# Inverting the 32x32 blocks of the WKV recurrence: the substitution on Pool over 128 partitions in place of VectorE in two halves

## The chip, the cores and the metric

The kernel runs on one core of a Trainium2 chip. Its engines are TensorE (PE, matrix products), VectorE (DVE), ScalarE (ACT), GpSimd (called Pool in the profile) and SyncE (SP), which here only issues DMAs. The metric is the device time of one execution in microseconds; the median of several runs is compared.

## The reference, cut to what matters

The kernel computes two blocks of a network on 1024 tokens of width 1024. The second block has, beside an attention branch and gates, a recurrence (WKV) over 8 heads of 64 channels. For each head a 64x64 state is carried over the tokens:

```python
def step(state, inp):
    r_t, d_t, k_t, v_t, a_t, b_t = inp
    sa = jnp.einsum('bhvk,bhk->bhv', state, a_t)
    state = (state * d_t[:, :, None, :] + sa[..., None] * b_t[:, :, None, :]
             + v_t[..., None] * k_t[:, :, None, :])
    return state, jnp.einsum('bhvk,bhk->bhv', state, r_t)
...
_, ys = lax.scan(step, jnp.zeros((B, H, N, N), jnp.float32), xs)
```

## The kernel before

All matrices are float32. Large products are made of three products each (`mm3`, L139 to L141): a weight is split into a high part by ScalarE (L103) and a low part by VectorE (L104). The weights go through two buffers each (`wr`, `wh`, `wl`), so that one unit of such a product (48 matmuls of 128x512) needs one load, one cast and one split.

The recurrence is computed in chunks of 64 tokens, and four chunks of all 8 heads make a time block; there are four time blocks, `tb` = 0 to 3. The function `rwkv` (L954) steps through generators. For each block, `wkv_prep` loads the inputs, scales them, normalises the keys (L1011 to L1021, with a reciprocal on VectorE at L1015) and multiplies them into 64x128 matrices `at` (L1114, masked at L1116). `wkv_inverse` inverts the 64x64 triangular part of each, first its 32x32 diagonal blocks: 32 pairs of head and chunk with two diagonal blocks each. `wkv_chain` then carries the state through the four chunks (L1193 to L1213), and `wkv_out` (L1225 to L1231) finishes.

The diagonal blocks go through DRAM (`dg`, stored at L1119), so that they can be loaded with one block's matrix in each partition: `d` and `tt` hold 128 partitions, one for a block, and matrix entries along the free axis. Each block is inverted by substitution in 31 steps; step j takes one product (L1144, into `tmp`) and one sum (L1145, into `tt`). The step works on n x m entries for each partition, with n = j // 2 + 1 and m = 31 - j; each step needs the one before. Partitions 0 to 63 and 64 to 127 have instructions of their own (`q` = 0 and 1). The results go back through DRAM (L1147), a transposed copy (`tn`, L1148) through `t11` (L1150), and are loaded at L1155 and L1159 into the layout that TensorE's products take (L1168 and L1174).

While a block is prepared and inverted, TensorE has other work: `projections` makes the latents and 16 gates (21 units of products of `hn`, into DRAM `cl` and `gd`). It follows the loop in the program; the functions' order in the program is a priority, and a planner that knows a cost for each instruction lays out a fixed order for each engine before the run. An engine works through its queue in that order and does not pass a waiting instruction. Loads and stores of this part are issued by SP, in a fixed order as well: the weights' loads (L129) and the stores at L1119, L1147 and L1150 share that queue.

Pool sets constants: `tt` to zero (L1132) and its diagonal to one (L1136), one column of `P` in each preparation (L1042), and later, in the attention, copies of keys (L784). All large tiles come from one pool of 38 slots, which limits how far a block can be prepared ahead.

Of the kernel before, what the change touches and what calls it, by code (L numbers as in the profile page):

```python
# [13 lines left out]
ALU = mybir.AluOpType  # L14
PSUM = bass.MemoryType.PSUM

P = 128
# [31 lines left out]
class Kernel:  # L49
# [1073 lines left out]
    def wkv_inverse(self, tb, live):  # L1123

        nc = self.nc
        ar, at, bt, uv, bv, dp = live

        tz = self.slot("d")
        d = tz.rearrange("p (j i) -> p j i", j=32)
        ts = self.slot("tt")  # L1130
        tt, tn = ts[:, 0:H].rearrange("p (k i) -> p k i", k=16), ts[:, H:2 * H].rearrange("p (i k) -> p i k", i=32)
        nc.gpsimd.memset(ts[:, 0:H], 0.0)  # L1132
        live.append(ts)
        pr = [(q, r, 64 * q + 32 * r) for q in range(2) for r in range(2)]
        for q, r, o in pr:
            nc.gpsimd.memset(ts[o:o + 32, r:512:34], 1.0)  # L1136
            nc.sync.dma_start(d[o:o + 32], self.dg[tb, q].rearrange("b e c a j i -> (b e c a) j i"))
        tmp = self.tp.tile([P, 144], F32, tag="wt3", name=self.nm("wt3"), bufs=1)
        for j in range(31):
            n, m = j // 2 + 1, 31 - j  # L1140
            for q in range(2):
                h = slice(64 * q, 64 * q + 64)
                t3 = tmp[h, 0:n * m].rearrange("p (k i) -> p k i", k=n)
                nc.vector.tensor_tensor(t3, d[h, j:j + 1, j + 1:32].to_broadcast([64, n, m]), tt[h, 0:n, j:j + 1].to_broadcast([64, n, m]), ALU.mult)  # L1144
                nc.vector.tensor_tensor(tt[h, 0:n, j + 1:32], tt[h, 0:n, j + 1:32], t3, ALU.add)  # L1145
        for q, r, o in pr:
            nc.sync.dma_start(self.dg[tb, q].rearrange("b e c a (k r) i -> r (b e c a) k i", r=2)[r], tt[o:o + 32])  # L1147
        nc.vector.tensor_copy(tn, tt.rearrange("p k i -> p i k"))  # L1148
        for q, r, o in pr:
            nc.sync.dma_start(self.t11[tb, q].rearrange("e c a i (r k) -> r (e c a) i k", r=2)[r], tn[o:o + 16])  # L1150
        t11, zs = (tz[:, i * H:i * H + H].rearrange("p (c a s) -> p c a s", c=4, a=4) for i in range(2))
        blk = lambda e, b: slice(64 * (1 - e) + 32 * b, 64 * (1 - e) + 32 * b + 32)
        for q in range(2):
            for e in range(2):
                nc.sync.dma_start(t11[blk(e, 0), 2 * q:2 * q + 2].rearrange("p c a s -> p (c a) s"), self.t11[tb, q, e].rearrange("c a i s -> i (c a) s"))  # L1155
        for c in range(4):
            for e in range(2):
                for b in range(2):
                    nc.sync.dma_start(at[c][blk(e, b), e, :, 32 * b:32 * b + 32], self.dg[tb, c // 2, b, e, c % 2].rearrange("a s i -> s a i"))  # L1159

        for q in range(2):
            yield
            cs = slice(2 * q, 2 * q + 2)
            pz, pw = (x.rearrange("p (c a s) -> p c a s", c=2, a=4) for x in self.halves(self.chain()))
            for c in range(2):
                for pt in range(4):
                    for e in range(2):
                        nc.tensor.matmul(pz[blk(e, 1), c, pt, :], lhsT=at[2 * q + c][blk(e, 0), e, pt, 32:64], rhs=t11[blk(e, 0), 2 * q + c, pt, :], start=True, stop=True)  # L1168
            for e in range(2):
                nc.scalar.copy(zs[blk(e, 1), cs].rearrange("p c a (k r) -> p (c a) r k", r=2), pz[blk(e, 1)].rearrange("p c a (r k) -> p (c a) r k", r=2))  # L1170
            for c in range(2):
                for pt in range(4):
                    for e in range(2):
                        nc.tensor.matmul(pw[blk(e, 0), c, pt, :], lhsT=zs[blk(e, 1), 2 * q + c, pt, :], rhs=at[2 * q + c][blk(e, 1), e, pt, 32:64], start=True, stop=True)  # L1174
                for e in range(2):
                    nc.vector.tensor_copy(at[2 * q + c][blk(e, 0), e, :, 32:64], pw[blk(e, 0), c])
# [324 lines left out]
```

## Time and profile before

| | us |
|---|---|
| median of 3 runs | 3022.22 |
| lowest and highest | 3017.02, 3025.08 |
| the profiled execution, its own time | 3025.18 |
| its span, first to last instruction | 3023.3 |
| TensorE busy | 2899.8 (96%) |
| VectorE busy | 1404.1 (46%) |
| ScalarE busy | 825.3 (27%) |
| Pool busy | 21.8 (1%) |

The profile is of one execution. Times are microseconds from the span's start unless marked ns. A row of the trace names the line of the code, the engine, the operation, the tile written and the tiles read, and the shape for a partition; "x62" is a count. The granted clock of TensorE is a share of its full speed, 2.4 GHz; 0.5 is the lower level, 1.2 GHz. A wait is put down to the event that ended it.

### The profile page before, as it was taken

To read this page: it belongs to the slowest core of one execution; us is meant where nothing else is said; L and a number is where in the kernel's file an instruction comes from. 1 tells how busy PE (TensorE), PEld (TensorE's weight loads), DVE (VectorE), ACT (ScalarE), POOL (GpSimd) and SP (SyncE) were. 2 spreads that over 40 slices of the span, in tenths; PEclk is the share of its full clock that TensorE was granted. 3 is DMA by queue.
4 is the path that set the end of the run, shared out by engine and by line. 5 is a ranking of instruction groups with operands and counts; after the bars stand their busy time and mean duration, and the time that the engine had idled before them with its cause. 6 is when DMAs were issued, how large, how long until landed. Compare 5 with 4: busy or idle time off the path is not lost.

```text
span 3023.3 us, 36716 instructions
## 1 busy us (share of the span) xinstructions
PE 2899.8 (96%) x15289; PEld 2327.6 (77%) x15289; DVE 1404.1 (46%) x2469; ACT 825.3 (27%) x1229; POOL 21.8 (1%) x73
## 2 busy tenths in 40 slices
PE   8989999999999999989788999999999999999998
PEld 6777888888888877867566777777888888888877
DVE  7774422222222462276676436545453333333366
ACT  4242311211121344143342334432131221111142
POOL 0000000000000000000000000000000000000000
PEclk9999999999999998999899999999999999999999
DMA  3344111111111234233232320023211111111122
GB/s 133 105 128 146 35 42 42 63 44 40 42 63 49 73 137 153 105 117 90 69 90 88 98 83 13 29 105 134 75 35 42 42 56 49 56 49 42 42 77 98
DMA packets 126390, 225.37 MB, mean 75 GB/s; under 512 B 52177, under 2 KB 73297, under 8 KB 126225
## 3 DMA queue, kind: packets, MB, share of 16 engines
q1 hardware_dynamic: 117200, 211.00, 21.0%
q10 hardware_dynamic: 9024, 12.04, 1.5%
q8 instruction: 120, 1.97, 0.3%
q14 instruction: 46, 0.37, 0.0%
HBM read 171.48 MB, written 48.23 MB: 73 GB/s over the span
## 4 chain that ended last, share of the span: by engine, by line
PE 87%; DVE 9%; issue 2%; ACT 1%; DMA 1%; ACTq 0%; SPq 0%; DVEq 0%
PE big L139 24%; PE big L140 24%; PE big L141 24%; PE big L822 2%; PE chain L855 2%; DVE tt L1145 2%; DVE wt L1144 2%; PE ps L839 1%; PE ps L1114 1%; PE ps L1021 1%; PE big L192 1%; PE chain L1205 0%; PE chain L139 0%; PE chain L140 0%; PE chain L141 0%
## 5 line engine op out<-in xcount | busy, mean ns | idle before, releaser
L139 PE MATMUL big<-hn,wh 128*128 128x512 f32 x1872 | 745.6, 399 | 8.5 <-DVE zo L914 4.0
L141 PE MATMUL big<-hn,wl 128*128 128x512 f32 x1872 | 742.5, 397 | 5.3 <-DVE wl L104 5.2
L140 PE MATMUL big<-hn,wh 128*128 128x512 f32 x1872 | 744.5, 398 | 1.9 <-DVE hn L197 1.9
L139 PEld LDWEIGHTS big<-hn,wh 128*128 128x128 f32 x1872 | 352.8, 189 | 94.2 <-issue 6.2
L141 PEld LDWEIGHTS big<-hn,wl 128*128 128x128 f32 x1872 | 353.4, 189 | 90.7 <-DVE wl L104 8.4
L140 PEld LDWEIGHTS big<-hn,wh 128*128 128x128 f32 x1872 | 353.0, 189 | 88.0 <-issue 3.2
L103 ACT CAST wh<-wr 128x1024 fp32r<-128x1024 f32 (+1 forms) x142 | 141.9, 1000 | 966.4 <-PE big L140 777.4
L104 DVE TENSOR_TENSOR wl<-wr,wh 128x1024 fp32r<-128x1024 f32 (+1 forms) x142 | 165.0, 1162 | 410.5 <-ACT wh L103 405.7
L140 PE MATMUL big<-wk,a 128*128 128x512 f32 x864 | 338.4, 394 | 0.0
L141 PE MATMUL big<-wk,a 128*128 128x512 f32 x864 | 338.3, 393 | 0.0
L139 PE MATMUL big<-wk,a 128*128 128x512 f32 x864 | 334.9, 396 | 1.8 <-ACT wk L103 1.8
L659 DVE TENSOR_TENSOR r<-big,r 128x1024 f32<-128x1024 f32 x144 | 176.2, 1224 | 318.2 <-PE big L141 318.1
L139 PEld LDWEIGHTS big<-wk,a 128*128 128x128 f32 x864 | 160.9, 188 | 43.8 <-ACT wk L103 7.6
L140 PEld LDWEIGHTS big<-wk,a 128*128 128x128 f32 x864 | 162.2, 188 | 38.8 <-DVE wk L104 0.7
L141 PEld LDWEIGHTS big<-wk,a 128*128 128x128 f32 x864 | 162.2, 188 | 37.6
L674 ACT ACTIVATE zo<-big 128x1024 f32<-128x1024 f32 x32 | 32.8, 1026 | 371.4 <-PE big L141 371.4
L668 DVE TENSOR_TENSOR zo<-zo,big 128x1024 f32<-128x1024 f32 x22 | 26.9, 1221 | 205.2 <-PE big L141 205.2
L104 DVE TENSOR_TENSOR wk<-wr,wk 128x1024 fp32r<-128x1024 f32 (+1 forms) x86 | 100.3, 1171 | 31.1 <-ACT wk L103 31.0
L140 PE MATMUL big<-wk,mx 128*128 128x512 f32 x256 | 102.3, 399 | 1.3 <-DVE wk L104 1.3
L139 PE MATMUL big<-wk,mx 128*128 128x512 f32 x256 | 101.0, 401 | 2.3 <-ACT wk L103 2.3
L141 PE MATMUL big<-wk,mx 128*128 128x512 f32 x256 | 101.6, 397 | 0.0
L675 DVE TENSOR_TENSOR zo<-zo 128x1024 f32<-128x1024 f32 x32 | 39.2, 1225 | 131.7 <-ACT zo L674 131.7
(411 smaller groups left out, 3629.5 us busy)
## 6 DMA issues: line engine op xcount, KB each, us to landing
wr<-in_w_ffn_up_dram SPq DMA_DIRECT2D x32, 512.0 KB, 3.2
wr<-in_w_ffn_down_dram SPq DMA_DIRECT2D x32, 512.0 KB, 3.2
zr<-zo SPq DMA_DIRECT2D x24, 512.0 KB, 3.5
wr<-in_w_gate_dram SPq DMA_DIRECT2D x22, 512.0 KB, 3.3
wr<-in_w_up_dram SPq DMA_DIRECT2D x22, 512.0 KB, 3.2
wr<-in_w_down_dram SPq DMA_DIRECT2D x22, 512.0 KB, 3.2
wr<-in_w_gates_dram SPq DMA_DIRECT2D x16, 512.0 KB, 4.9
gd<-zo SPq DMA_DIRECT2D x16, 512.0 KB, 3.0
```

The source lines that it names most:

```text
L103: nc.scalar.copy(hi, x)
L104: nc.vector.tensor_tensor(lo, x, hi.bitcast(F32), ALU.subtract)
L139: nc.tensor.matmul(ps, lhsT=w[0], rhs=x[0], start=start, stop=False)
L140: nc.tensor.matmul(ps, lhsT=w[0], rhs=x[1], start=False, stop=False)
L141: nc.tensor.matmul(ps, lhsT=w[1], rhs=x[0], start=False, stop=stop)
L659: nc.vector.tensor_tensor(res[t], ps, res[t], ALU.add)
L674: nc.scalar.activation(s, ps, AF.Relu)
L675: nc.vector.tensor_tensor(s, s, s, ALU.mult)
L822: nc.tensor.matmul(sc[:, c:c + m], lhsT=qs[e][:, i * P:(i + 1) * P], rhs=ks[e][:, c:c + m], start=True, stop=True)
L855: nc.tensor.matmul(o, lhsT=pts[t // 4][:, (t % 4) * P:(t % 4 + 1) * P], rhs=vh, start=t == 0, stop=t == i)
L1144: nc.vector.tensor_tensor(t3, d[h, j:j + 1, j + 1:32].to_broadcast([64, n, m]), tt[h, 0:n, j:j + 1].to_broadcast([64, n, m]), ALU.mult)
L1145: nc.vector.tensor_tensor(tt[h, 0:n, j + 1:32], tt[h, 0:n, j + 1:32], t3, ALU.add)
```

## The change

The loop over the two halves is gone: each of the 31 steps has one product and one sum over all 128 partitions, and they are issued to Pool, as is the transposed copy `tn`. What is computed stays the same, and so do the loads and stores around it.

```diff
--- before.py
+++ after.py
@@ -1138,14 +1138,12 @@
         tmp = self.tp.tile([P, 144], F32, tag="wt3", name=self.nm("wt3"), bufs=1)
         for j in range(31):
             n, m = j // 2 + 1, 31 - j
-            for q in range(2):
-                h = slice(64 * q, 64 * q + 64)
-                t3 = tmp[h, 0:n * m].rearrange("p (k i) -> p k i", k=n)
-                nc.vector.tensor_tensor(t3, d[h, j:j + 1, j + 1:32].to_broadcast([64, n, m]), tt[h, 0:n, j:j + 1].to_broadcast([64, n, m]), ALU.mult)
-                nc.vector.tensor_tensor(tt[h, 0:n, j + 1:32], tt[h, 0:n, j + 1:32], t3, ALU.add)
+            t3 = tmp[:, 0:n * m].rearrange("p (k i) -> p k i", k=n)
+            nc.gpsimd.tensor_tensor(t3, d[:, j:j + 1, j + 1:32].to_broadcast([P, n, m]), tt[:, 0:n, j:j + 1].to_broadcast([P, n, m]), ALU.mult)
+            nc.gpsimd.tensor_tensor(tt[:, 0:n, j + 1:32], tt[:, 0:n, j + 1:32], t3, ALU.add)
         for q, r, o in pr:
             nc.sync.dma_start(self.dg[tb, q].rearrange("b e c a (k r) i -> r (b e c a) k i", r=2)[r], tt[o:o + 32])
-        nc.vector.tensor_copy(tn, tt.rearrange("p k i -> p i k"))
+        nc.gpsimd.tensor_copy(tn, tt.rearrange("p k i -> p i k"))
         for q, r, o in pr:
             nc.sync.dma_start(self.t11[tb, q].rearrange("e c a i (r k) -> r (e c a) i k", r=2)[r], tn[o:o + 16])
         t11, zs = (tz[:, i * H:i * H + H].rearrange("p (c a s) -> p c a s", c=4, a=4) for i in range(2))
```

## Rows read from the trace of the kernel before

**Rows 1.** Profile page: busy time and count of each engine; granted clock in 40 slices.

```profile
PE 2899.8 (96%) x15289; PEld 2327.6 (77%) x15289; DVE 1404.1 (46%) x2469; ACT 825.3 (27%) x1229; POOL 21.8 (1%) x73
...
PEclk9999999999999998999899999999999999999999
```

**Rows 2.** Table by stretch, one for each time block's inversion; columns in its first line.

```profile
core 0: us, PE busy (x) PEld busy (x) DVE busy (x) ACT busy (x) POOL busy (x), PEclk, DMA share, GB/s
1324.00:1416.00 92.00, 77.17 (x781) 60.47 (x781) 65.30 (x182) 27.93 (x50) 1.01 (x5) 0.89 0.35 100
1416.00:1526.00 110.00, 93.15 (x934) 70.57 (x934) 77.93 (x215) 40.34 (x67) 1.14 (x6) 0.91 0.31 89
1526.00:1632.00 106.00, 91.29 (x961) 70.25 (x956) 73.95 (x192) 39.30 (x66) 1.15 (x6) 0.95 0.31 94
1632.00:1726.00 94.00, 81.78 (x776) 61.84 (x772) 49.00 (x146) 24.91 (x38) 0.00 (x0) 0.93 0.25 73
```

**Rows 3.** Table by stretch inside the first time block, the same columns.

```profile
1320.00:1345.00 25.00, 25.00 (x131) 20.34 (x130) 19.30 (x73) 9.95 (x16) 0.00 (x0) 1.00 0.56 171
1345.00:1367.00 22.00, 9.33 (x33) 6.59 (x31) 20.31 (x60) 6.28 (x6) 0.00 (x0) 0.61 0.14 36
1367.00:1390.00 23.00, 20.84 (x125) 15.61 (x126) 16.45 (x29) 7.04 (x13) 0.00 (x0) 0.93 0.30 70
```

**Rows 4.** Waits of PE, 1284 to 1780 us: us in total, times, longest.

```profile
PE ps L1021 <- DVE rn L1015: 43.0, 6, 10.9
PE big L141 <- DVE wl L104: 5.2, 2, 5.0
```

**Rows 5.** Timeline, ACT and DVE, 1332 to 1367 us: start, duration, work.

```profile
1332.09 1.05 ACT L103 CAST wh<-wr 128x1024 fp32r<-128x1024 f32 x1 [10.02 <-PE big L140]
...
1365.83 1.22 DVE L104 TENSOR_TENSOR wl<-wr,wh 128x1024 fp32r<-128x1024 f32 x1
```

**Rows 6.** Groups of DVE instructions by line, 1324 to 1680 us.

```profile
L1144 DVE TENSOR_TENSOR wt<-d,tt 64x126 f32<-64x126 f32 (+19 forms) x248 | 62.0, 250 | 8.6 <-DMA d<-dg_wkv 0.9
L1145 DVE TENSOR_TENSOR tt<-tt,wt 64x126 f32<-64x126 f32 (+19 forms) x248 | 61.9, 250 | 8.1
```

**Rows 7.** Table by stretch, the first inversion: every engine.

```profile
1324.00:1375.00 51.00, 38.22 (x170) 29.90 (x170) 45.92 (x147) 15.87 (x23) 0.00 (x0) 0.83 0.37 113
```

**Rows 8.** First and last inversion: their start, and TensorE's first use (L1168).

```profile
L1144 DVE TENSOR_TENSOR wt<-d,tt x62: 177/258/297, 1324.8 to 1372.4; 64x126 f32<-64x126 f32 x6, 64x30 f32<-64x30 f32 x4, 64x56 f32<-64x56 f32 x4, 64x78 f32<-64x78 f32 x4
L1168 PE MATMUL chain<-d,at x32: 191/191/212, 1390.3 to 1391.7; 32*32 32x32 f32 x32
L1144 DVE TENSOR_TENSOR wt<-d,tt x62: 177/258/298, 1626.3 to 1673.6; 64x126 f32<-64x126 f32 x6, 64x30 f32<-64x30 f32 x4, 64x56 f32<-64x56 f32 x4, 64x78 f32<-64x78 f32 x4
L1168 PE MATMUL chain<-d,at x32: 191/191/212, 1687.1 to 1688.6; 32*32 32x32 f32 x32
```

**Rows 9.** Pool: groups by line, then two rows of its timeline.

```profile
L784 POOL COPY kh<-kpe 64x512 f32<-64x512 f32 x16 | 10.5, 665 | 287.1 <-DMA kpe<-rope 162.2 <-PE ps L839 74.0 <-PE chain L855 50.2
...
L507 POOL MEMSET pl_s<- 128x16 f32 x10 | 1.1, 111 | 16.5 <-DVE t L160 8.4 <-DVE pl_s L508 4.8 <-DVE pl_d L513 1.3
...
1294.62 0.64 POOL L1136 MEMSET tt<- 32x16 f32 x4
...
1422.03 0.13 POOL L1042 MEMSET P<- 128x16 f32 x1 [15.76 <-PE chain L1205]
```

**Rows 10.** SP queue: DMAs of the inversion by line, and the wait at L1147.

```profile
L1147 SPq DMA_DIRECT2D dg_wkv<-tt x16: 549/569/2008, 1357.8 to 1675.0; - x16
L1150 SPq DMA_DIRECT2D t_wkv<-tt x16: 549/618/627, 1375.2 to 1677.8; - x16
L1159 SPq DMA_DIRECT2D at<-dg_wkv x64: 343/430/451, 1360.8 to 1687.9; - x64
DMA to landing us min/median/max: 1.6/1.8/3.5
SPq L1147 <- DVE tt L1145: 61.9, 7, 20.9
```

## The prediction

> **What bounds the kernel now.** I read the profile from the outside in. The page says that TensorE (PE) is busy for 2899.8 of 3023.3 us and that VectorE (DVE) has 1404.1 us of work and Pool 21.8 [rows 1]. So the kernel is bound by TensorE, and a change can win only where TensorE stands still or runs at the low clock. The clock row dips only around the middle, so the next view is the table by stretch over the four time blocks in which the 32x32 blocks are inverted. In 92, 110, 106 and 94 us TensorE is busy for 77.17, 93.15, 91.29 and 81.78: it is idle for 14.8, 16.9, 14.7 and 12.2 us, together 58.6 [rows 2]. The finer table of the first block puts nearly all of that into one place: TensorE is full from 1320 to 1345, then works 9.33 of 22 us while DVE is busy for 20.31 of them [rows 3]. The waits of TensorE say for whom: 43.0 us for the reciprocal of L1015 and 5.2 us for the weight split of L104, both on DVE [rows 4].
>
> Neither of these belongs to the inversion. They are late because DVE is held by it. The timeline shows it on one weight: ScalarE writes the high part (L103) at 1332.09, and DVE makes the low part (L104) only at 1365.83, 33 us later, for 1.22 us of work [rows 5]. In between stand the 31 steps of the substitution, two instructions each for two halves of the partitions. The planner put them first on DVE's queue, the preparation of the next time block and the splits of the gate weights behind them; TensorE's fill runs dry, because each unit of fill needs one split.
>
> The idle stretches also cost clock. From 1345 to 1367 the granted clock is 0.61, a mixture of the two levels 2.4 and 1.2 GHz. Busy time times the missing clock is 9.33 x 0.39 = 3.6 there and 20.84 x 0.07 = 1.5 from 1367 to 1390 [rows 3]. The coarse row of that block would give 77.17 x 0.11 = 8.5, so 60% of the coarse figure falls on work. The four coarse figures are 8.5, 8.4, 4.6 and 5.7 [rows 2], together 27; 60% is 16 us. At most 58.6 + 16 = 75 us are there to be won. I expect 48.2 of the 58.6 idle (the two named waits) and the same share of the clock, 13, to go: 61 us. The rest hangs on ScalarE and on issue.
>
> **What is removed.** Both lines have 248 instructions on DVE, 62.0 and 61.9 us [rows 6], and with them four copies (L1148). That is about 125 us less on DVE. DVE is not the bound, so the number itself buys nothing; what counts is that a split or a reciprocal no longer queues behind some 31 us of it in each block (62.0 + 61.9, over 4).
>
> **What is added on Pool.** For each block 62 instructions on 128 partitions, each needing the one before, and a copy. The elements per partition are (j // 2 + 1) x (31 - j); over j = 0 to 30 that is 2856, twice 5712, on average 92 in an instruction. The trace has no Pool instruction with two inputs, so I bound the price by its neighbours [rows 9]. Four memsets of 32x16 that write into one tile take 0.64 us, 0.16 each: the fixed part of a short one. From the memset of 16 columns (111 ns) to the copy of 512 (665 ns) it is 1.12 ns for an element with one input. Below: 62 x 0.16 + (5712 - 62 x 16) x 1.12 ns = 9.9 + 5.3 = 15 us. With two inputs read in turn the slope doubles: 9.9 + 10.5 = 20 us. Starting two reads and handing the result to the next instruction is not in any row; one more fixed part each, from 0.1 to 0.2 us, adds 6 to 12. So 26 to 33 us for a Pool left alone, 29 in the middle. Above, the farthest row is DVE's own inversion, 1324.8 to about 1374, 50 us [rows 8]. The Trainium skill, "GPSIMD Engine Reference" section 3.1, gives 4497 ns for a two-input add of 2048 elements on Pool against 2293 on VectorE; by that rate, an estimate, the element part would be 12.5 us in place of 10.5, 8 us more in the sum, and no row here shows it. DVE's remaining work may also be in Pool's way; in the first inversion DVE is busy for 45.92 us [rows 7], 14.9 of them not the inversion's 31. I take 6 of these, because the rows cannot show a hold-up: 35 us for a block, ends 15 and 50.
>
> **When is Pool fast enough?** TensorE works in order; it comes to the inverse's first product (L1168) and stands there if the result is late, with all the fill behind it. In the first block the product follows the start of the inversion by 1390.3 - 1324.8 = 65.5 us, in the last by 60.8 [rows 8]. Without the losses of those blocks (14.8 + 5 and 12.2 + 3) TensorE would be there after about 45 us. Of these the way back through DRAM takes a part. All of it now starts after the last step, since the first half is no longer finished before the second: four stores at L1147 (0.57 each) and four at L1150 (0.62), half of the 16 loads at L1159 (0.43) and two or three landings of 1.8 [rows 10], about 13 us with the copy. That leaves 45 - 13 = 32 us for Pool. Every microsecond above 32 is waited for four times; at 35 us that is 4 x 3 = 12.
>
> **The sum.** 3025.18 (the profiled execution, 2 us of it outside the span) - 61 + 12 = 2976. The median of the three runs is 3 us below the profiled one, so 2973.
>
> **The queues passed.** The loads of d and the stores stay on SP. SP waited 61.9 us in seven waits at L1147 for the end of the inversion [rows 10], with the loads of weights (L129) queued behind; if Pool ends earlier than DVE did, this wait shrinks, if later it grows, and TensorE's fill then lacks weights as well as splits. On Pool the memset of the next block's P (L1042, 0.13 us) comes 5 us after the second inversion's start [rows 9] and will stand among Pool's steps: at worst the next preparation waits for the inversion, as it does now on DVE. That I cost at nothing, since DVE's own queue is its cover today. The copies of L784 come 100 us after the last inversion and meet nothing.
>
> **The rivals.**
> 1. Pool and DVE hold each other up. Pool would then be slowed by all of DVE's remaining work: 29 + 14.9 = 44 us, TensorE waits 4 x 12 = 48, and 3025 - 61 + 48 = 3012, 3009 as a median. For it speaks that the work released on DVE (preparation, splits) moves exactly into Pool's time, and nearly all of it reads two tiles. The Trainium skill, "SBUF — State Buffer", section "Who interferes with whom", says that a VectorE instruction with two SBUF inputs contends with a GpSimd instruction that reads SBUF, and that the loser is blocked for the whole of the other; the trace of before has no such pair, so it neither agrees nor disagrees.
> 2. Slower: TensorE stands at L1168 for a late Pool. It decides from the length of one inversion: 3025 - 61 + 4 x (I - 32) passes 3025 at I = 47 and is slower by what can be told (0.3%, 9 us) from I = 49.5. At 0.85 us an instruction, I = 53: 3025 - 61 + 84 = 3048, 3045 as a median. The same happens with a Pool as fast as I think if the planner counts on a still shorter one and puts L1168 earlier on TensorE's queue: each microsecond earlier costs four. For it: a chain of dependent short instructions on an engine that has hardly worked in this kernel. Against it: 62 instructions in place of 124, and now 50 us are used.
> 3. No change: I between 45 and 49.5, or TensorE still stands at the reciprocal, since prepared data for it come as late as before. About 3020.
>
> **How the numbers follow.** Forecast, a Pool chain of 26 to 38 us: 0.45, from 2955 to 2985. Rival 1: 0.25, from 2985 to 3012. Rival 3: 0.12. Rival 2: 0.18. The first two are faster by over 0.3% (about what a measurement here can tell from no change): 0.70; within 0.3%: 0.12; slower: 0.18. The range reaches from 2945 (all of the 75 won, as a median, and little more) to 3033 (I = 50); it leaves out most of rival 2.
>
> **What would show it.** Right: in the same stretches TensorE's idle of 58.6 falls below 20, no wait for L1015, the split follows its ScalarE half within 2 us, and Pool has 248 instructions of about 0.45 to 0.55 us, start to start. Rival 1: the start-to-start time on Pool is long only where DVE works. Rival 2: a wait of TensorE at L1168, and of SP at L1147, for Pool. The prediction fails if one inversion on Pool takes more than 45 us, or if the planner's new order leaves TensorE idle elsewhere.

## The result, and the profile after

The changed kernel takes 2988.41 us in the median of 4 runs (2985.46 to 2991.03), the kernel before 3023.65; the ratio is 0.9887, 95% interval 0.9868 to 0.9906. It is 35 us faster, where 49 were forecast (2973).

The page of the changed kernel, busy time of each engine:

```profile
PE 2895.4 (97%) x15289; PEld 2324.7 (78%) x15289; DVE 1279.9 (43%) x1969; ACT 821.2 (28%) x1227; POOL 136.2 (5%) x325
```

TensorE has the same 15289 products and nearly the same busy time as before; VectorE (DVE) has 124 us less and Pool 114 more, so the work moved as described [rows 1, 6]. The table by stretch of the changed kernel, each stretch from the start of one inversion to the next, the last to the end of its recurrence (columns as in [rows 2]):

```profile
1324.00:1414.00 90.00, 89.80 (x848) 72.10 (x847) 38.12 (x71) 32.03 (x55) 31.85 (x70) 0.96 0.38 110
1414.00:1514.00 100.00, 91.59 (x976) 69.80 (x975) 44.07 (x68) 37.53 (x68) 29.54 (x70) 0.95 0.35 104
1514.00:1608.00 94.00, 85.72 (x863) 65.36 (x863) 40.91 (x62) 36.05 (x62) 29.30 (x69) 0.95 0.32 95
1608.00:1686.00 78.00, 71.66 (x728) 54.85 (x729) 19.05 (x31) 20.02 (x32) 26.92 (x62) 0.93 0.25 75
```

The four blocks take 362 us in place of 402 [rows 2]. TensorE is idle for 0.2, 8.4, 8.3 and 6.3 us, together 23.2 in place of 58.6. So 35 us of idle are gone, as much as the medians differ by. (The two profiled executions are 39.7 us apart; the rest, 4.4, is TensorE's busy time, 2899.8 before and 2895.4 after.) What is left is named, for the most part, by one wait of TensorE (1284 to 1780 us; total, times, longest):

```profile
PE chain L1166 <- DMA d<-t_wkv: 20.3, 3, 7.5
```

The two waits of [rows 4] are gone. A new one stands in their place: TensorE waits three times for the way back of the inverse, at the inverse's first product (L1168 before the change, L1166 after; every line behind the loop moves up by two). On the timeline of the changed kernel the split that stood 33 us behind its ScalarE half [rows 5] now follows it at once:

```profile
1330.15 1.05 ACT L103 CAST wh<-wr 128x1024 fp32r<-128x1024 f32 x1 [10.01 <-PE big L140]
...
1331.24 1.45 DVE L104 TENSOR_TENSOR wl<-wr,wh 128x1024 fp32r<-128x1024 f32 x1 [1.56 <-ACT wh L103]
```

The groups of Pool's products and copies, by line (busy us, mean ns); the sums of L1143 are 124 more, of 441 ns:

```profile
L1142 POOL TENSOR_TENSOR wt<-d,tt 128x126 f32<-128x126 f32 (+22 forms) x124 | 55.2, 445 | 73.2 <-DMA d<-dg_wkv 63.8
...
L1146 POOL COPY tt<-tt 128x512 f32<-128x512 f32 x4 | 4.4, 1102 | 0.3
```

One inversion, from the first product's start to the last sum's end, lasts 34.2, 32.2, 32.0 and 30.8 us, 32.3 in the mean, in place of about 50 [rows 8].

### The profile page after: what moved, and what is told of

Read it like the earlier page. It is cut to its first block, busy times and chain, and to the rows that moved or that the text cites. A ratio compares the mean times of both kernels' runs of the same rounds, so it can differ in the third digit from the quotient of the medians.

```text
span 2983.7 us, 36459 instructions
## 1 busy us (share of the span) xinstructions
PE 2895.4 (97%) x15289; PEld 2324.7 (78%) x15289; DVE 1279.9 (43%) x1969; ACT 821.2 (28%) x1227; POOL 136.2 (5%) x325
## 4 chain that ended last, share of the span: by engine, by line
PE 87%; DVE 4%; POOL 3%; DMA 2%; ACT 2%; issue 2%; SPq 0%; ACTq 0%; DVEq 0%; POOLq 0%
PE big L139 25%; PE big L140 25%; PE big L141 24%; PE big L822 2%; PE chain L855 2%; POOL tt L1143 1%; POOL wt L1142 1%; PE ps L839 1%; PE ps L1114 1%; PE big L192 0%; PE chain L139 0%; DMA x<-in_x_dram 0%; ACT hn L195 0%; PE chain L141 0%; PE chain L140 0%
## 5 line engine op out<-in xcount | busy, mean ns | idle before, releaser
L104 DVE TENSOR_TENSOR wl<-wr,wh 128x1024 fp32r<-128x1024 f32 (+1 forms) x142 | 165.6, 1167 | 431.5 <-ACT wh L103 430.9
L104 DVE TENSOR_TENSOR wk<-wr,wk 128x1024 fp32r<-128x1024 f32 (+1 forms) x86 | 100.2, 1171 | 31.6 <-ACT wk L103 31.6
L103 ACT CAST wk<-wr 128x1024 fp32r<-128x1024 f32 (+1 forms) x86 | 85.2, 1001 | 44.2 <-DMA wr<-in_w_out_dram 36.0
```

What stands on the lines that cost most here:

```text
L103: nc.scalar.copy(hi, x)
L104: nc.vector.tensor_tensor(lo, x, hi.bitcast(F32), ALU.subtract)
```

## The experiments

Two questions were open: what of the gain comes from moving the work to Pool and what from making one instruction of two halves, and why TensorE waits for Pool although its chain is as short as forecast.

Each edit gets an order of its own from the planner, so a difference between two kernels is that of the edit and of its order together.

**The two halves of the change apart.** The first kernel is the kernel before with the loop of the substitution alone edited, the second the changed kernel with the loop alone edited. Each cut below shows the kernel against the other of these two, so that the line of the copy stands in it as well. First, one instruction for all partitions, on VectorE (against the changed kernel):

```diff
-            nc.gpsimd.tensor_tensor(t3, d[:, j:j + 1, j + 1:32]...
-            nc.gpsimd.tensor_tensor(tt[:, 0:n, j + 1:32], ...
+            nc.vector.tensor_tensor(t3, d[:, j:j + 1, j + 1:32]...
+            nc.vector.tensor_tensor(tt[:, 0:n, j + 1:32], ...
-        nc.gpsimd.tensor_copy(tn, ...
+        nc.vector.tensor_copy(tn, ...
```

> Only one half of the change is made: the two halves become one instruction over 128 partitions, and VectorE keeps the work. Theory (what counted was how long VectorE is held in one piece, not that it is free of this work): 62 instructions of 0.25 us with 0.06 between them hold it for about 20 us a block instead of 50, no longer than the fill that TensorE has in hand, so the waits for L1015 and L104 all but go and no result is late; 2950 to 2970 us. Rival (VectorE must be free of the work): the split still queues behind the inversion, a third or more of the 48 us of waits stays, and the time is 2985 to 3005 us.

2978.91 us (2977.39 to 2981.77), ratio 0.9852, interval 0.9838 to 0.9867. It lies between the two expectations, and it is faster than the changed kernel. The group of VectorE's products in this kernel (the sums are 124 more, of 249 ns), then its table by stretch:

```profile
L1142 DVE TENSOR_TENSOR wt<-d,tt 128x126 f32<-128x126 f32 (+22 forms) x124 | 30.9, 249 | 3.4 <-DMA d<-dg_wkv 0.9
```

```profile
1323.00:1422.00 99.00, 96.20 (x903) 75.73 (x902) 50.94 (x135) 32.63 (x56) 1.01 (x5) 0.95 0.36 106
1422.00:1517.00 95.00, 92.75 (x914) 70.20 (x913) 54.62 (x130) 38.61 (x66) 1.14 (x6) 1.00 0.38 112
1517.00:1607.00 90.00, 80.33 (x853) 59.87 (x852) 52.42 (x127) 35.53 (x62) 1.14 (x6) 0.94 0.34 95
1607.00:1686.00 79.00, 79.00 (x802) 60.70 (x800) 35.01 (x96) 23.91 (x38) 0.00 (x0) 1.00 0.30 92
```

An instruction over 128 partitions takes 249 ns; one over 64 took 250 [rows 6]. So joining the halves removes half of the work, 62 us, at no price. TensorE is idle for 2.8, 2.3, 9.7 and 0 us, 14.7 in all. More than half of it is one wait, where the theory had expected no late result (total, times, longest):

```profile
PE ps L1002 <- DVE r L1081: 8.1, 2, 8.0
```

An inversion here lasts 43, 45, 41 and 27 us from the first block to the last, though its 62 instructions are only 15 us of work: the planner put preparation and splits between its steps, and they are not late.

Second, the work on Pool, in two halves as before (against the kernel before):

```diff
-                nc.vector.tensor_tensor(t3, d[h, j:j + 1, j + 1:32]...
-                nc.vector.tensor_tensor(tt[h, 0:n, j + 1:32], ...
+                nc.gpsimd.tensor_tensor(t3, d[h, j:j + 1, j + 1:32]...
+                nc.gpsimd.tensor_tensor(tt[h, 0:n, j + 1:32], ...
-        nc.vector.tensor_copy(tn, ...
+        nc.gpsimd.tensor_copy(tn, ...
```

> Only the other half of the change is made: the work goes to Pool, in two halves of 64 partitions as before. Theory (TensorE waits in order for a late result, four times for every microsecond): 124 instructions of 0.36 us and a gap of up to 0.08 make an inversion of 48 to 60 us, 13 to 25 longer than now, so the time is 3040 to 3090 us and the wait at the first product of the inverse grows by that much in each block. Rival (the planner knows the longer chain and puts more fill before the product): no more than 3005 us.

3096.09 us (3094.54 to 3099.34), ratio 1.024, interval 1.0225 to 1.0255. The move alone makes the kernel 73 us slower. Its group of Pool's products (the sums have another 248), and TensorE's wait:

```profile
L1144 POOL TENSOR_TENSOR wt<-d,tt 64x126 f32<-64x126 f32 (+17 forms) x248 | 99.5, 401 | 103.8 <-DMA d<-dg_wkv 85.3
```

```profile
PE chain L1168 <- DMA d<-t_wkv: 128.9, 4, 35.0
```

Twice the instructions make an inversion of 56.2 to 59.9 us, 58.2 in the mean, 26 more than in the changed kernel. TensorE's wait goes from 20.3 to 128.9 us, 27 more a block, and the time rises by 108: four for each microsecond, as the theory says. Counted in the timeline, TensorE has 98 to 121 of the fill's products between the inversion's start and the first product, against 102 to 142 in the changed kernel, and comes to that product 31.3 to 34.3 us after the start, against 32.2 to 42.6. For an inversion 26 us longer the planner put no more fill in front.

The one on VectorE and the changed kernel were run once more side by side.

> The changed kernel once more, to stand beside the next one on the same chip: 2985 to 2992 us by both theories.

> The substitution on VectorE over 128 partitions once more. Theory (one instruction for both halves is what pays, Pool adds nothing to it): 2977 to 2982 us, 7 to 12 us under the changed kernel, with intervals that do not meet. Rival (the two ways are the same within what can be told): within 5 us of the changed kernel.

2986.96 us (2982.72 to 2989.90; ratio 0.9879, interval 0.9864 to 0.9894) for Pool and 2976.98 (2976.10 to 2978.63; 0.9847, 0.9833 to 0.9862) for VectorE. The intervals just miss each other: the VectorE version with joined halves is 10 us the faster and beats both the kernel before and the changed one.

**A longer chain on Pool.** The line with the product stands twice:

```diff
             nc.gpsimd.tensor_tensor(t3, d[:, j:j + 1, j + 1:32]...
+            nc.gpsimd.tensor_tensor(t3, d[:, j:j + 1, j + 1:32]...
```

> The changed kernel with each product of the substitution issued twice on Pool: 31 instructions more in a block, each 0.36 us and a gap of 0.08, 13 us a block, and nothing else. Theory (four times for every microsecond): 2988 + 4 x 13 = 3040 us. Rival (the planner counts the longer chain and fills): 2990 to 3005 us.

3021.32 us (3017.25 to 3024.73), ratio 0.9995, interval 0.9985 to 1.0004. It lies between the two. The inversions last 50.7, 46.3, 49.3 and 44.8 us, 15.5 more in the mean. The wait:

```profile
PE chain L1167 <- DMA d<-t_wkv: 51.3, 4, 18.9
```

51.3 in place of 20.3 us is 7.7 more a block, half of the 15.5. Here 129 to 138 products of fill stand before the first product, in place of 102 to 142 with three of the four up, and TensorE comes to it 52.1, 41.9, 38.3 and 39.1 us after the inversion's start, in place of 42.6, 33.4, 32.2 and 32.3: 7.7 later in the mean, the other half. So the new order makes room for half of what was added, and for none of it in the second kernel above. What TensorE waits is not the chain's length over a fixed limit; it looks like the real length less the length planned. That is argued: what the planner reckons for these instructions is in no trace, nor why it made room here and not there.

**A shorter way back.** The stores at L1145 and every second load at L1157 go to ScalarE's DMA queue:

```diff
-            nc.sync.dma_start(self.dg[tb, q]...
+            nc.scalar.dma_start(self.dg[tb, q]...
-                    nc.sync.dma_start(at[c][blk(e, b), e, :, ...
+                    (nc.sync, nc.scalar)[b].dma_start(at[c][blk(e, b), e, :, ...
```

> The changed kernel with half of the inverse's way through DRAM on ScalarE's DMA queue: the four stores of the inverse and half of the sixteen loads back. Theory (TensorE waits 20 us in three blocks for the last part of the way, most of it issue time on one queue): the way is 3 to 4 us shorter, the wait falls to about 10 us, 2973 to 2982 us. Rival (ScalarE's queue stands at the stores for Pool, with its casts and evacuations behind it): slower than 2990, up to 3030 us.

3027.42 us (3025.93 to 3030.44), ratio 1.0014, interval 1.0004 to 1.0023: the rival. TensorE's first product comes 6.5 to 7.0 us after the inversion's end, where it was 7.7 to 8.5, so the way is about 1 us shorter and not 3 to 4. The order is another one too: TensorE comes to that product 27 to 36 us after the inversion's start, where it was 32 to 43. TensorE's waits, and ScalarE's waits behind the loads:

```profile
PE chain L1166 <- DMA d<-t_wkv: 28.6, 4, 8.6
PE ps L1002 <- issue: 15.3, 2, 8.5
```

```profile
ACT tt L995 <- DMA at<-dg_wkv: 38.1, 2, 20.6
...
ACT tt L995 <- DMA d<-t_wkv: 19.1, 1, 19.1
ACT r L995 <- DMA at<-dg_wkv: 18.1, 1, 18.1
```

The scaling of L995 stands on ScalarE's queue behind the inverse's loads, which wait for their stores; four of them cost ScalarE 75 us. TensorE now waits in four blocks for the inverse, and for other work too; that the 15.3 us at L1002 come from ScalarE's queue is likely, but the profile names no releaser for them.

**The copy back on VectorE.**

```diff
-        nc.gpsimd.tensor_copy(tn, ...
+        nc.vector.tensor_copy(tn, ...
```

> One part of the change undone: the transposed copy is VectorE's again, the steps stay on Pool. Theory (the copy of 1.1 us on Pool lies beside the four stores at L1145, 2.6 us of issue on SP): no change, 2986 to 2991 us. Rival (it is on the way to the first product): 0.5 us in each of three blocks and more where VectorE is busy, 2980 or 2995.

2999.21 us (2994.66 to 3001.68), ratio 0.9919, interval 0.9904 to 0.9933: 12 us slower than the changed kernel run beside it, and more than the rival's 2995. Waits of TensorE, waits of VectorE, and two rows of VectorE's timeline in the third block:

```profile
PE big L141 <- DVE wl L104: 11.3, 1, 11.3
PE ps L1021 <- DVE rn L1015: 8.8, 1, 8.8
```

```profile
DVE tt L1146 <- POOL tt L1143: 51.8, 4, 17.0
```

```profile
1551.94 0.60 DVE L1146 COPY tt<-tt 128x512 f32<-128x512 f32 x1 [16.98 <-POOL tt L1143]
1552.45 1.22 DVE L104 TENSOR_TENSOR wl<-wr,wh 128x1024 fp32r<-128x1024 f32 x1
```

The copy itself takes 0.60 to 0.64 us in place of 1.1 on Pool. But it waits on VectorE's queue for Pool's last step, 51.8 us in four blocks, and what is queued behind it waits as well: in the third block the split of L104 follows the copy at once, and TensorE, which needs it, stands for 11.3 us until 1553.72. The waits for L104 and L1015 are back, and the wait for the inverse falls from 20.3 to 5.8 us. That the change moved the copy too was a part of its gain.

**No substitution.** The loop of 31 steps is left out.

```diff
-        for j in range(31):
-            ...
```

> The 31 steps are left out, so that the blocks are not inverted; loads, stores, copy and products stay. It shows what the inversion costs in all. Theory (75 us was all that idle and low clock of TensorE could give; without steps nothing is left to wait for but the way through DRAM): 2945 to 2955 us. Rival (the planner puts the first product so much earlier that TensorE now waits for the way through DRAM, 5 us a block, and the low clock of the small products stays): 2960 to 2975 us.

2981.30 us (2972.65 to 2988.35), ratio 0.9860, interval 0.9837 to 0.9884. With no inversion at all the kernel is no faster than with the joined one on VectorE (2979 and 2977). Its table by stretch:

```profile
1322.00:1409.00 87.00, 81.10 (x870) 66.31 (x868) 34.33 (x59) 30.43 (x56) 2.80 (x7) 0.90 0.33 98
1409.00:1505.00 96.00, 90.58 (x825) 69.46 (x825) 42.96 (x76) 38.34 (x63) 2.44 (x6) 0.95 0.34 100
1505.00:1595.00 90.00, 86.59 (x891) 66.19 (x892) 41.50 (x64) 37.03 (x63) 2.21 (x7) 0.98 0.37 106
1595.00:1670.00 75.00, 75.00 (x829) 57.09 (x825) 24.07 (x40) 26.65 (x44) 0.00 (x0) 1.00 0.33 96
```

TensorE is still idle for 5.9, 5.4, 3.4 and 0 us, 14.7 in all, and the clock is under its upper level in three of the stretches. The rival's time is nearer, and of its two reasons one: the low clock stays (14.2 us, counted as in the next section), but no wait for the way through DRAM is left among TensorE's waits.

**Do Pool and VectorE hold each other up?** A section in front of the changed kernel runs 32 dependent Pool instructions on 128x128 four times; beside them VectorE does nothing, or eight instructions of one kind on 128x1024, with short ones of the program's own between them:

```python
kinds = (None,
         lambda: nc.vector.tensor_tensor(f, d, e, ALU.mult),       # d, e in SBUF
         lambda: nc.vector.tensor_tensor(f, d, ps, ALU.mult),      # ps in PSUM
         lambda: nc.vector.tensor_scalar(f, d, 2.0, None, ALU.mult),
         lambda: nc.vector.tensor_tensor(f, d, e, ALU.mult))       # without Pool
```

> The changed kernel with a measured section in front: 32 dependent Pool instructions on 128x128 (alternately product and sum) four times, beside eight VectorE instructions on 128x1024 that are, in turn, absent, with two inputs from SBUF, with one input from SBUF and one from PSUM, and with one input alone; then eight with two SBUF inputs without Pool. Theory (Pool and VectorE hold each other up where VectorE reads two SBUF tiles, and only there): Pool alone 0.42 to 0.46 us an instruction; beside two SBUF inputs some Pool instructions last 1.2 us or more and the VectorE ones 1.3 to 1.6 in place of 1.22; beside a PSUM input as alone. With one SBUF input open: as alone if VectorE then reads by its own path. Rival (any VectorE work slows Pool, by memory traffic): all three are slower alike.

Rows of Pool's timeline in one execution, one from each part: alone, beside two SBUF inputs, beside one from PSUM, beside one input alone.

```profile
25.34 0.45 POOL L1372 TENSOR_TENSOR mb_y<-mb_x,mb_t 128x128 f32<-128x128 f32 x1
...
31.63 1.44 POOL L1373 TENSOR_TENSOR mb_t<-mb_t,mb_y 128x128 f32<-128x128 f32 x1
...
62.49 0.46 POOL L1372 TENSOR_TENSOR mb_y<-mb_x,mb_t 128x128 f32<-128x128 f32 x1
...
78.41 0.86 POOL L1372 TENSOR_TENSOR mb_y<-mb_x,mb_t 128x128 f32<-128x128 f32 x1
```

The VectorE rows of the last three:

```profile
33.01 1.21 DVE L1363 TENSOR_TENSOR mb_f<-mb_d,mb_e 128x1024 f32<-128x1024 f32 x1
36.53 1.47 DVE L1363 TENSOR_TENSOR mb_f<-mb_d,mb_e 128x1024 f32<-128x1024 f32 x1
...
63.30 1.21 DVE L1364 TENSOR_TENSOR mb_f<-mb_d,big 128x1024 f32<-128x1024 f32 x1
...
76.31 0.82 DVE L1365 TENSOR_SCALAR mb_f<-mb_d 128x1024 f32<-128x1024 f32 x1
```

Alone a Pool instruction takes 0.45 us (from 18.97 us on, where VectorE has nothing left of its own). While VectorE reads two SBUF tiles, eight of the first nine take 1.31 to 1.44, about one VectorE instruction and a little more; while VectorE reads one tile and PSUM it takes 0.45 to 0.47 but for one of 1.00, which lies beside an instruction of the program's own with one SBUF input (L180). One SBUF input alone is not harmless: 0.79 to 0.92 on Pool, and on VectorE 0.82 in three of eight, in place of 0.68. VectorE with two SBUF inputs pays less: one of eight takes 1.47, the others 1.21 to 1.22. The theory holds for two SBUF inputs and for PSUM; its "only there" does not. The rival (any VectorE work, by memory traffic) falls by the PSUM part.

## Why the prediction was right, and where it was not

**The time against its bands.** The median of 2988 lies above the band of the forecast (2955 to 2985) and in that of rival 1 (2985 to 3012), but not by rival 1's chain of 44 us: an inversion takes 32.3, as the forecast had it (26 to 38). Of the forecast's own signs, idle below 20 us was missed (23.2), and rival 2's sign, a wait at the inverse's first product, is there.

**What bounds it: right.** The 43.0 and 5.2 us of [rows 4] were VectorE's queue behind the inversion; they are gone in the changed kernel and in the one with joined halves on VectorE, and they come back when a copy on VectorE waits for Pool.

**The idle: right in sum, by luck.** Forecast were 48 us of idle gone and 12 of waiting new, 36 in all; measured were 58.6 - 23.2 = 35.4. But the new wait is 20.3, 8 more than forecast, and 7.5 us of the rest, which I had left to ScalarE and issue, went too. The two misses cancel.

**The clock: the step that failed.** I took 13 us of clock to come back with the idle, and priced the new wait at its idle alone. Busy time times the missing clock, summed over the four blocks in steps of 2 us, is 14.5 us in the kernel before and 14.4 after (16.0 in the second trace of the changed kernel): nothing came back there. The 13 us are nearly the whole of the 15 (2988 less 2973) by which the forecast was off. (Between the two profiled executions the miss is 9.5: outside the four blocks, where nothing was changed, the same sum is 28.8 before and 24.8 after.) Rows of the changed kernel's table show why:

```profile
1388.00:1392.00 4.00, 4.00 (x38) 3.57 (x36) 1.83 (x2) 1.12 (x3) 0.00 (x0) 1.00 0.36 111
1392.00:1396.00 4.00, 4.00 (x35) 3.42 (x34) 2.52 (x10) 0.00 (x0) 0.00 (x0) 0.53 0.16 37
1448.00:1452.00 4.00, 0.00 (x0) 0.00 (x0) 0.00 (x0) 0.00 (x0) 0.00 (x0) 0.79 0.46 67
1452.00:1456.00 4.00, 2.52 (x52) 2.27 (x52) 0.00 (x0) 0.00 (x0) 0.00 (x0) 0.50 0.37 57
1456.00:1460.00 4.00, 4.00 (x22) 3.30 (x22) 0.00 (x0) 1.12 (x3) 0.00 (x0) 0.50 0.17 25
```

The late inverse at 1453 leaves TensorE idle for 6.5 us; the granted clock falls to 0.5, the lower level, and TensorE then works its next stretch of full load at it, to about 1460. The three waits of 6.3 to 7.5 us bring three such stretches, with 3.5, 3.0 and 4.4 of the 14.4 us; the other 3.4 come from 1392 on, where the clock falls without idle. Before, the granted clock stood at the lower level for 65 us of the four blocks, and TensorE was busy in 29 of them; after, it is 29 of 38. So the low level lasts for less time, and is filled with as much work. The joined kernel on VectorE, with one wait of 8.0 us in place of the three, loses 7.6 us (9.2 in its second trace): there a part of the clock did come back. The share of the clock's loss that "falls on work" is no constant, as I used it.

**Pool's price: right.** Alone 29 us were forecast. The instruction of 16 elements takes 0.23 us and that of 136 takes 0.45:

```profile
1331.68 1.25 POOL L1142 TENSOR_TENSOR wt<-d,tt 128x115 f32<-128x115 f32 x1
...
1338.95 0.45 POOL L1143 TENSOR_TENSOR tt<-tt,wt 128x136 f32<-128x136 f32 x1
...
1346.85 0.39 POOL L1142 TENSOR_TENSOR wt<-d,tt 128x110 f32<-128x110 f32 x1
...
1358.24 0.23 POOL L1143 TENSOR_TENSOR tt<-tt,wt 128x16 f32<-128x16 f32 x1
```

Each instruction taken at the shortest time that it has in any of the four blocks sums to 22.2 us; with the gaps of 0.08 between them that is 27. The fixed part lies within what I had (0.2 us and a gap of 0.08, against 0.16 and 0.1 to 0.2 more), the slope is smaller (some 1.8 ns an element, 0.22 us over 120 elements, where I had 2.24). What an inversion takes above the 27 is the hold-up, which I had put at 6 us: 7.1, 5.1, 4.9 and 3.8 us, and 20.6 of these 21 us lie in Pool instructions that overlap one of VectorE's with two SBUF inputs. (The forecast's side estimate of 12.5 us counted all 5712 elements, and the 10.5 beside it 4720; over the same elements the two are 10.4 and 10.6.) In the same timeline the product at 1331.68 takes 1.25 us, beside VectorE's split at 1331.24, and the one at 1346.85 takes 0.39 beside a VectorE instruction that reads PSUM:

```profile
1346.75 0.69 DVE L1053 TENSOR_TENSOR kk<-kk,ps 128x512 f32<-128x512 f32 x1 [0.75 <-PE ps L1021]
```

So rival 1's mechanism is there; its size, up to 14.9 us, was too large: a VectorE instruction of 1.45 us cost Pool 0.85 (1.25 in place of some 0.40), not its whole length, since Pool's had started 0.44 us after it and ended 0.24 after its end; and a VectorE instruction that reads PSUM cost it nothing. The rule of the Trainium skill that I cited with it ("SBUF — State Buffer", "Who interferes with whom") agrees with the measured section: two SBUF inputs 1.44 us, a PSUM input 0.45, alone 0.45.

**When Pool is fast enough: two errors that cancel in part.** I had TensorE at the first product 45 us after the inversion's start, and a way back of 13. The timeline of TensorE in the changed kernel, at the second inversion, which started at 1413.60 and ended at 1445.83:

```profile
1453.48 0.31 PE L1166 MATMUL chain<-d,at 32*32 32x32 f32 x2 [6.46 <-DMA d<-t_wkv]
```

TensorE was there at 1447.0, 33.4 us after the start, in the new order of the planner; the way back took 7.7. SP's queue shows what I had counted too much: the product follows the first loads of `t11`, issued from 1451.52 on, when one of the sixteen loads of L1157 has been issued and not eight; and Pool's copy (1.13 us from 1445.89) lies beside the first four stores (2.58 us from 1445.86). The limit for Pool was then 33.4 - 7.7 = 25.7 and not 32, and the wait 6.5 and not 3, in three blocks of four; in the first TensorE comes after 42.6 us and does not wait. The sentence that each microsecond is waited for four times held with the halves on Pool (108 us for 26) and not with the doubled product (33 for 15.5, two for each). What decides is, as far as these runs tell, what the forecast named as a second way of rival 2: how far the planner's length falls short.

**At most 75 us: too wide a bound.** These were all the idle and low clock of the four blocks. The kernel without steps wins 42: 14.7 us of idle and 14.2 of low clock are left in it though nothing is substituted. The joined kernel on VectorE, which wins 45, keeps 14.7 us of idle as well. So not all of the 75 was the inversion's to give back.

**Not priced at all: the joining.** The sum took the change as one move. Its parts apart are 45 us faster (joined, on VectorE) and 73 us slower (moved, in halves); together 35 faster, so they do not add up. The gain is the joining's; once the halves are joined, the move takes 10 of it back. The trace of before had the price, and I didn't ask for it. The groups of VectorE between 1284 and 1780 us, on 64 and on 128 partitions:

```profile
L1077 DVE TENSOR_TENSOR bk<-a,sg 64x512 f32<-64x512 f32 x16 | 11.0, 686 | 0.3
L1066 DVE TENSOR_TENSOR ar<-kk,P 128x512 f32<-128x512 f32 x8 | 5.2, 685 | 0.1
```

With 512 columns each, 64 partitions take 686 ns and 128 take 685: twice the partitions cost nothing, so half of the 124 us of [rows 6] was to be saved where they were.

**The queues: right for Pool, wrong for SP.** No engine waits for Pool's memset of P in the trace. SP's wait at its first store was to shrink if Pool ended earlier than VectorE did. An inversion is 17 us shorter, and the wait is no shorter, 65.8 us in four blocks where it was 61.9 in seven [rows 10]:

```profile
SPq L1145 <- POOL tt L1143: 65.8, 4, 19.0
```

It did no harm: TensorE's waits for weights are at most 0.4 us.

## What to carry to other kernels

Before moving a chain of short instructions to another engine, count what joining them over the partitions gives where they are: the instruction's time hardly depended on the number of partitions (249 and 250 ns on VectorE; on Pool, at 126 entries and at the shortest, 407 over 128 and 399 over 64). When a chain moves, look where the engine that needs its result will stand in the new order: here it came to the product after 32 us for a chain and a way back of 40, and a margin was missing. What depends on the chain has to move with it, or the old engine's queue stands behind it (51.8 us for one copy). And idle time that is won need not bring clock back: here the idle went from 58.6 to 23.2 us, and the clock's loss stayed at 14.4. A new wait is to be priced with the low clock that follows it.

## What the runs showed of the hardware that was not expected

TensorE's granted clock fell where the profile shows the engine fully busy (it models where a product ends, so short gaps between small products would not show). In the rows of the table above it is 1.00 from 1388 to 1392 and 0.53 from 1392 to 1396, with 4.00 of 4.00 us busy in both; in the second trace of the changed kernel it is 0.63 from 1392 to 1396, with 4.00 busy. What TensorE did before are almost only small products of the recurrence, as its timeline shows:

```profile
1384.22 1.15 PE L1098 MATMUL ps<-cst,v 128*64 128x64 f32 x32
...
1388.84 1.95 PE L1248 MATMUL big<-cst,zo 128*128 128x1 f32 x16
...
1392.90 2.66 PE L1114 MATMUL ps<-ar,bk 64*128 64x128 f32 x16
...
1397.47 1.79 PE L1098 MATMUL ps<-cst,v 128*64 128x64 f32 x28
```

The first is 32 products of 128x64 after a run of fill that ends at 1384, then come products of 128x128, 64x64, 64x128 and one column, with a single one of the fill, at 1390.65. The 32 products at 1384.22 took 1.15 us, 28 of the same at 1397.47 took 1.79: 36 ns each and 64. The kernel without substitution has one such fall too, at 1410.6, after 12.5 us of which TensorE is busy for 12.46. Why the clock falls there was not tried.

A VectorE instruction with a single SBUF input and no PSUM (tensor_scalar on 128x1024) also held Pool up, to 0.79 to 0.92 us from 0.45, and itself took 0.82 in place of 0.68. I had taken two SBUF inputs to be the condition. The same section of the Trainium skill lists tensor_scalar among the instructions that can take the pair of ports which VectorE shares with GpSimd, when its operands allow a mode that uses both. The run agrees in so far as Pool was held up; which mode VectorE ran in, it does not show.
